# A hybrid decoder trunk on one NeuronCore: output projection and second norm by pairs of row tiles, and one list schedule to the end

## The chip, the cores and the metric

The kernel runs on one core of a Trainium2 chip. The metric is the device time of one execution in microseconds. A profiled execution gives a trace; its span is the time between the first and the last instruction in it.

## The reference

One layer on x of 1024 rows (tokens) by 1024 columns, all in float32:

```python
h = rms_norm(x, norm_mix)
xa, ga, q, f, v, g, m_a, m_b = split(h @ w_in)            # eight groups of 1024 columns
y_a = rg_lru(conv(xa)) * gelu(ga)                         # a gated linear recurrence over the rows
y_b = rms_norm(hgrn2(silu(q), f, v), hg_norm) * silu(g)   # 8 heads, a recurrence with a 128x128 state
y = sigmoid(m_a) * y_a + sigmoid(m_b) * y_b
x = x + y @ w_out                                         # the output projection
h = rms_norm(x, norm_mlp)                                 # the second norm
x = x + square(relu(h @ w_up)) @ w_down                   # w_up 1024x4096, w_down 4096x1024
out = rms_norm(x, norm_final)
```

## The kernel before

**Stages.** Columns stand on partitions in the mixer, rows (tokens) in the output projection. (1) The first norm and the projection of v. (2) The mixer: 28 quads, blocks of 256 columns of w_in, each multiplied in 7 products instead of 8 (a scheme after Strassen over two halves of the rows, two of the contraction and two of the columns), beside it the recurrences of `gated_recurrence` (4) and `hgrn` (8 heads), and `merge(u)`, which makes y of 128 columns, `u`, in two halves of 512 rows, `c`, and stores it to DRAM as `y_d[u, c]`. (3) The output projection `y @ w_out` with the residual, and the second norm, its result transposed and split into the seven operands of the MLP. (4) UP: 16 quads of w_up, 84 matmuls each (`hidden`), whose results go to DRAM. (5) DOWN: 8 rounds (`kb`) of two quads of w_down, added to eight accumulators `acc`, and the last norm.

**Exact products.** A float32 operand is split into a rounded high part H on ACT (`A.copy`) and a rest L on VectorE (`split`); a product is three matmuls, H by H, H by L and L by H (`mm3`).

**Weights.** A tile of w_out (two blocks of 128 rows by 512 columns) is 512 KB. It goes through one of three raw buffers and is split into one of three pairs H and L. `next_w` walks a fixed list, `seq`: the eight tiles three times, 24 loads and splits.

**Stage 3 before.** Row tiles are 128 rows; `tt` numbers them within a half of 512 rows, `t` over both (0 to 7), `hf` is a half of the 1024 result columns. First the first half: `load_y(0)` brings eight y tiles of 512 KB, four row tiles together accumulate in four PSUM banks over eight blocks `ku`, once for each `hf`, and the sums with x go to DRAM (`x2d`). Then `load_y(1)`, and in two parts: two row tiles of the first half are read back (`x2a`) and normed, then two row tiles of the second half are projected and normed. The norm of a row tile is a square with its sum (ACT), a power (POOL), a scaling (VectorE, `xn`), eight transposes (`xT_h`, TensorE), copies out of PSUM (`braw`), and splits; once both halves are there, `combos` makes the four combined operands. In PSUM there are four banks `pj`, two `sc`, two `hg`.

**What sets the order.** In the mixer each instruction is noted by class `Later` rather than issued: `note` finds what it depends on, `cost` estimates its length, `ordered` walks forward in estimated time and takes on each engine the ready instruction with the earliest due time, and `issue` emits the list. Each engine runs its queue in order, and SP's queue of DMAs too. From stage 3 on, before, the framework's scheduler orders the instructions by program order and priority.

**Memory.** Before, each stage opens pools of its own, and the mixer's tiles (its operands `hop`) are closed ahead of stage 3.

Of the kernel before, what the change touches and what calls it, by code (L numbers as in the profile page):

```python
# [11 lines left out]
F32 = mybir.dt.float32  # L12
F32R = mybir.dt.float32r
U8 = mybir.dt.uint8
AF = mybir.ActivationFunctionType
# [4 lines left out]
P = 128  # L20
# [36 lines left out]
class Later:  # L57
# [7 lines left out]
    TABLE = 1.28  # L65
# [11 lines left out]
    class Pool:  # L77
        def __init__(self, later, real):
            self.later, self.real = later, real

        def tile(self, shape, dtype, *, tag, name, bufs=1, **k):
            t = self.real.tile(shape, dtype, tag=tag, name=name, bufs=bufs, **k)
            ring = self.later.rings.setdefault((id(self), tag), [])
            ring.append(t.tensor.name)
            if len(ring) > bufs:
                self.later.before[ring[-1]] = ring[-1 - bufs]
            return t

    def __init__(self, tc):
        self.tc, self.on, self.due = tc, False, 0.0  # L90
        self.rings, self.before = {}, {}
        self.ops, self.seen, self.of_tile = [], {}, {}
# [10 lines left out]
    def cost(engine, method, out, k, aps):  # L103
# [14 lines left out]
        if engine == "POOL":  # L118
            return (0.2 + 0.00075 * n if method == "memset" else 0.65 + 0.0009 * n), 0.12, 0
# [30 lines left out]
    def ordered(self):  # L150
# [5 lines left out]
        for name, before in self.before.items():  # L156
            if name in self.of_tile and before in self.of_tile:
# [3 lines left out]
                preds.append(set(self.of_tile[before]))  # L161
# [53 lines left out]
        while done < total:  # L215
# [22 lines left out]
        self.span, self.starts = max(free.values()), starts  # L238
# [12 lines left out]
def trunk(ctx: ExitStack, tc: tile.TileContext, x, wts, quads, pv, gains, mask_f, mask_u, out):  # L251
    nc = tc.nc
    later = Later(tc)
# [10 lines left out]
    wp, rawp, ps = (Later.Pool(later, p) for p in (wp, rawp, ps))  # L264
    dram = ctx.enter_context(tc.tile_pool(name="dram", bufs=1, space=DRAM))

    def opened(name, **how):
        cm = tc.tile_pool(name=name, bufs=1, reuse_waits="tile", **how)
        return Later.Pool(later, cm.__enter__()), lambda: cm.__exit__(None, None, None)
# [7 lines left out]
    seq = [*range(V_TILES), *range(V_TILES)] + [*range(out0, out0 + OUT_TILES)] * 3  # L277
# [21 lines left out]
    def split_w(i, raw):  # L299
        h = wp.tile([P, 1024], F32R, tag="w", name=f"wH{i}", bufs=6)  # L300
        lo = wp.tile([P, 1024], F32R, tag="w", name=f"wL{i}", bufs=6)
# [38 lines left out]
    def gain_tile(i, pool):  # L340
        g = pool.tile([P, D], F32, tag="gain", name=f"gain{i}")
        nc.scalar.dma_start(g, gains[i : i + 1, :].to_broadcast([P, D]))
# [79 lines left out]
    def quad_steps(i, pools, raws=raw_tile, singles=2, adding=False):  # L422
# [38 lines left out]
        def pair(src, names):  # L461
            def go():
                h, lo = (pools[1].tile([P, 1024], F32R, tag="w", name=f"w{names[0]}{i}{q}", bufs=6) for q in "HL")
# [14 lines left out]
            "b": pair(lambda: s[0], ("s1", "s2")),  # L478
            "c": pair(lambda: s[1], ("s3", "s4")),
            "d": pair(lambda: raw[1], ("A12", "A22")),  # L480
# [10 lines left out]
    FAR = ("t1L", "n2L", "T3L", "T4L")  # L491
    hop = {
        o: [
            (hopr if o + q in FAR else hopl).tile([P, 4, T], F32R, tag=o + q, name=f"h{o}{q}") for q in ("H", "L")
        ]
        for _, _, o in PLAN
    }
# [574 lines left out]
    later.on = True  # L1072
# [28 lines left out]
    ysp, close_ys = opened("ys")  # L1101
# [3 lines left out]
    n2p, close_n2 = opened("n2")  # L1105
    gain1 = gain_tile(1, n2p)
# [349 lines left out]
```

## Time and profile before

| | us |
|---|---|
| median of 3 runs | 1633.67 (1632.45 to 1635.85) |
| profiled execution | 1640.74 |
| its span | 1639.0 |
| TensorE busy | 1551.2, 8520 matmuls |
| VectorE / ACT / POOL busy | 1232.0 / 859.8 / 273.2 |
| moved by DMA | 320.98 MB, mean 196 GB/s |

In the profile, PE is TensorE's matmuls, PEld its weight loads, DVE VectorE, ACT ScalarE, POOL GpSimd and SPq the DMA issues of SyncE. A name such as `po<-wH,y` is the output tile and the inputs, without numbers: `po` is a bank of the output projection, `wH` and `wL` a split weight tile, `y` a tile of y, `mga`, `mgb`, `mgo`, `mgh` the tiles of `merge`, `yd`, `od`, `hd`, `mad`, `mbd` tensors in DRAM, `uX`, `uY`, `uZ` the banks of UP, `dX` and so on those of DOWN. A row of busy time by stretch gives its start and end, its length, then the busy time of each engine with the instructions that lie in it, the granted clock of TensorE as a share of full speed, the busy share of the DMA engines, and GB/s.

### The profile page before, as it was taken

To read this page: it belongs to the slowest core of one execution; us is meant where nothing else is said; L and a number is where in the kernel's file an instruction comes from. 1 tells how busy PE (TensorE), PEld (TensorE's weight loads), DVE (VectorE), ACT (ScalarE), POOL (GpSimd) and SP (SyncE) were. 2 spreads that over 40 slices of the span, in tenths; PEclk is the share of its full clock that TensorE was granted. 3 is DMA by queue.
4 is the path that set the end of the run, shared out by engine and by line. 5 is a ranking of instruction groups with operands and counts; after the bars stand their busy time and mean duration, and the time that the engine had idled before them with its cause. 6 is when DMAs were issued, how large, how long until landed. Compare 5 with 4: busy or idle time off the path is not lost.

```text
span 1639.0 us, 22939 instructions
## 1 busy us (share of the span) xinstructions
PE 1551.2 (95%) x8520; PEld 1238.0 (76%) x8520; DVE 1232.0 (75%) x1780; ACT 859.8 (52%) x1356; POOL 273.2 (17%) x281
## 2 busy tenths in 40 slices
PE   5999999999999999988898797999999999999997
PEld 4787878777778777776776575878778878888886
DVE  4754586978778778877892387977777888788876
ACT  4643666468455854488542266766766732222113
POOL 0001222334214522345232000000000000000000
PEclk9999999999999999998899898999999999999999
DMA  5546464565564565545558861666656575666652
GB/s 189 168 130 181 127 200 121 169 190 171 155 171 152 168 201 170 169 148 148 168 178 292 296 227 67 261 250 233 232 222 239 219 295 211 256 252 244 256 206 103
DMA packets 110801, 320.98 MB, mean 196 GB/s; under 512 B 11872, under 2 KB 20192, under 8 KB 99936
## 3 DMA queue, kind: packets, MB, share of 16 engines
q1 hardware_dynamic: 101040, 299.05, 51.2%
q0 software_dynamic: 8064, 14.68, 5.8%
q10 hardware_dynamic: 1584, 5.77, 1.0%
q8 instruction: 67, 1.10, 0.3%
q14 instruction: 46, 0.38, 0.1%
HBM read 217.75 MB, written 101.71 MB: 195 GB/s over the span
## 4 chain that ended last, share of the span: by engine, by line
PE 74%; DVE 9%; DMA 7%; ACT 6%; issue 3%; POOL 1%; SPq 0%; DVEq 0%; POOLq 0%; ACTq 0%
PE pQFX L247 5%; PE pGMX L247 5%; PE pGAX L247 4%; PE dX L327 4%; PE dX L329 4%; PE dX L328 4%; PE uX L327 3%; PE uX L328 3%; PE uX L329 3%; PE pGMY L247 3%; DMA raw<-wts_in 2%; PE pQFY L247 2%; PE sc L247 2%; PE pGAY L247 2%; PE dY L329 2%
## 5 line engine op out<-in xcount | busy, mean ns | idle before, releaser
L1371 DVE TENSOR_TENSOR acc<-acc,dX 128x512 f32<-128x512 f32 x128 | 85.2, 683 | 31.0 <-PE dX L329 29.9
L288 ACT CAST wA<-q 128x512 fp32r<-128x512 f32 x33 | 20.4, 621 | 139.4 <-PE dX L329 102.7
L289 DVE TENSOR_TENSOR wL<-raw,wH 128x1024 fp32r<-128x1024 f32 x40 | 49.9, 1250 | 31.7 <-ACT wH L288 29.0
L247 POOL DMA_DIRECT2D s<-quads_in x52 | 46.6, 901 | 158.7 <-DMA s<-quads_in 46.0
L288 ACT CAST wH<-raw 128x1024 fp32r<-128x1024 f32 x40 | 41.9, 1047 | 44.2 <-PE po L328 18.7
L247 ACT ACT_TABLE_LOAD x50 | 64.2, 1283 | 1.6 <-PE pi L247 0.7
L327 PE MATMUL po<-wH,y 128*128 128x512 f32 x128 | 52.1, 410 | 4.7 <-DMA y<-yd 4.7
L1371 DVE TENSOR_TENSOR acc<-acc,dY 128x512 f32<-128x512 f32 x64 | 43.5, 685 | 16.2 <-PE dY L329 15.4
L247 DVE TENSOR_TENSOR s<-s,q 128x512 f32<-128x512 f32 x54 | 43.5, 806 | 11.6 <-DMA s<-quads_in 8.1
L328 PE MATMUL po<-wL,y 128*128 128x512 f32 x128 | 52.1, 407 | 0.0
L329 PE MATMUL po<-wH,y 128*128 128x512 f32 x128 | 51.3, 402 | 0.0
L1230 ACT ACTIVATE b<-b 128x512 f32<-128x512 f32 x48 | 30.3, 631 | 37.4 <-DVE b L1229 37.4
L247 DVE TENSOR_TENSOR qb<-qb,seg 128x512 f32<-128x512 f32 (+1 forms) x40 | 27.3, 683 | 17.0 <-PE sc L247 16.2
L247 DVE TENSOR_TENSOR kk<-kk,seg 128x768 f32<-128x768 f32 (+1 forms) x32 | 29.3, 915 | 9.3 <-PE sc L247 9.3
L247 PEld LDWEIGHTS sc<-qb,kk 128*32 128x32 f32 (+1 forms) x896 | 21.3, 116 | 19.7 <-issue 16.6
L289 DVE TENSOR_TENSOR wA<-q,wA 128x512 fp32r<-128x512 f32 x33 | 22.6, 686 | 14.9 <-ACT wA L288 14.9
L327 PEld LDWEIGHTS po<-wH,y 128*128 128x128 f32 x128 | 25.1, 197 | 10.5 <-DMA y<-yd 5.3
L247 PE MATMUL sc<-qb,kk 128*32 128x48 f32 (+2 forms) x896 | 27.3, 211 | 4.8 <-DVE dd L247 2.4
L1231 ACT ACTIVATE b<-b 128x512 f32<-128x512 f32 x48 | 30.2, 631 | 1.3
L247 POOL TENSOR_SCALAR scT<-dd 32x256 f32<-32x256 f32 x32 | 19.9, 621 | 60.8 <-DVE dd L247 48.0
L1150 PE MATMUL xT_h<-ident,xn_h 128*128 128x128 f32 x64 | 10.7, 323 | 20.0 <-DVE xn_h L351 13.0
L329 PEld LDWEIGHTS po<-wH,y 128*128 128x128 f32 x128 | 25.2, 197 | 5.4
(3093 smaller groups left out, 5502.1 us busy)
## 6 DMA issues: line engine op xcount, KB each, us to landing
q<-quads_in SPq DMA_DIRECT2D x92, 512.0 KB, 4.5
raw<-wts_in SPq DMA_DIRECT2D x40, 512.0 KB, 4.7
s<-quads_in SPq DMA_DIRECT2D x56, 256.0 KB, 2.9
s<-quads_in POOLq DMA_DIRECT2D x56, 256.0 KB, 5.0
y<-yd SPq DMA_DIRECT2D x16, 512.0 KB, 5.9
q<-quads_in SPq DMA_DIRECT2D x28, 256.0 KB, 4.0
x<-x_in SPq DMA_DIRECT2D x8, 512.0 KB, 4.6
vd<-vt SPq DMA_DIRECT2D x16, 256.0 KB, 3.6
```

Source lines behind the costliest of these rows:

```text
L247: go(*a, **k)
L288: keep(A.copy(h, src))
L289: keep(V.tensor_tensor(out=lo, in0=src, in1=h.bitcast(F32), op=ALU.subtract))
L327: PE.matmul(o, ah, bh, start=first, stop=False, **how)
L328: PE.matmul(o, ah, bl, start=False, stop=False, **how)
L329: PE.matmul(o, al, bh, start=False, stop=last, **how)
L1150: PE.transpose(pt[:, k * P : (k + 1) * P], xn[:, (4 * h + k) * P : (4 * h + k + 1) * P], ident)
L1230: A.activation(b[:, at, :], b[:, at, :], AF.Relu, scale=-1.0 if at == 2 else 1.0)
L1231: A.activation(b[:, at, :], b[:, at, :], AF.Square)
L1371: V.tensor_tensor(out=dst, in0=dst, in1=banks[bk, pr], op=op)
```

## The change

1. `later.issue()` moves from the end of the mixer to the end of the kernel: mixer, output projection, second norm, UP and DOWN are noted and ordered in one list. New due times: `OUT_FROM` 690 and 12 us a pair, 2.85 a step in UP, 1.4 a step and row pair in DOWN.
2. Homes of 8 KB last from the mixer to the end. Tiles of the mixer's operands (`NEAR`) give their places to later tiles of the same pool: B11H, B11L and t1H to y (three homes, later the u tiles), n2H to x (later the sums of the quads), B21H to the gain and xn, B21L and T3H to `braw` (later UP's results, then four accumulators). `Pool.place` and `before` follow which tiles share bytes.
3. The output projection goes by pairs of row tiles, `tt` and `tt + 4`, one of each half, with both `hf` for a pair before the next. y comes in 64 loads of 128 KB (rows of 512 bytes) instead of 16 of 512 KB; x in 8 of 512 KB. The sums are normed from where they lie, and stored to DRAM for DOWN; they are not read back. The last pair finishes its first row tile ahead of its second.
4. Weight tiles of w_out are kept in three homes by last use (`w_of`); pairs walk the tiles back and forth. Loads and splits remain 24.
5. Estimates: a DMA takes 1.9 us and its size at 330 GB/s (190 before), 160 with accumulation; POOL's costs are new; SP is held when more than 3 us of transfers are under way by the estimate (`AHEAD`).

The diff, cut to its core:

```diff
-    TABLE = 1.28
+    TABLE, AHEAD = 1.28, 3.0
...
-            slow = "accum_op" in k
-            return (0.92 if engine == "POOL" else 0.06), 1.9 + size / (1.0e5 if slow else 1.9e5), size / 2.0e5
+            moved = size / (1.6e5 if "accum_op" in k else 3.3e5)
+            return (0.92 if engine == "POOL" else 0.06), 1.9 + moved, moved
...
                 moving = max(moving, at) + moved
+                free[e] = max(free[e], moving - self.AHEAD)
...
+    NEAR = {"B11H": "y0", "B11L": "y1", "t1H": "y2", "n2H": "x2", "B21H": "gx", "B21L": "b0", "T3H": "b1"}
...
+    near = Homes(y=("y0", "y1", "y2"), x2=("x2",), gx=("gx",), b=("b0", "b1"), u1=("gx",), u2=("y0", "y1", "y2"), s=("x2",))
...
-    later.issue()
-    for close in (close_m, close_w1m, close_hopl, close_ev, close_hopr, close_mk):
+    for close in (close_m, close_w1m, close_ev, close_hopr, close_mk):
         close()
...
+    gx = near.tile([P, 2, D], F32, tag="gx", name="gx")
+    gain1, xn = gx[:, 0, :], gx[:, 1, :]
+    HIDDEN_PACE, DOWN_PACE, OUT_PACE, OUT_FROM = 2.85, 1.4, 12.0, 690.0
+    def w_of(hf, j):
+        if (hf, j) not in out_w:
+            home = used_at.index(min(used_at))
...
+            raw = load_w(i)
+            pair = [wp.tile([P, 1024], F32R, tag=f"w{home}{q}", name=f"w{q}{i}_{made[0]}") for q in "HL"]
+            split(raw, *pair)
...
-    ys = load_y(0)
-    for hf in range(2):
-        pp = out_proj(ys, hf, range(4), "0")
-        for tt in range(4):
-            cols = slice(hf * 512, (hf + 1) * 512)
-            xs = n2p.tile([P, D], F32, tag="xn", name=f"xs{tt}{hf}", bufs=2)[:, 0:512]
-            SP.dma_start(xs, x[tt * P : (tt + 1) * P, cols])
-            V.tensor_tensor(out=xs, in0=pp[tt], in1=xs, op=ALU.add)
-            SP.dma_start(x2d[tt][:, cols], xs)
-    ys = load_y(1)
-    for part in range(2):
-        tts = (2 * part, 2 * part + 1)
-        for tt in tts:
...
-            second_norm(tt, 0)
-        for hf in range(2):
-            pp = out_proj(ys, hf, tts, "1")
...
-        for tt in tts:
-            SP.dma_start(x2d[4 + tt], x2s[tt])
-            second_norm(tt, 1)
+    later.due = OUT_FROM
+    for tt in range(4):
+        js = range(4) if tt == 0 else range(3, -1, -1)
+        for n, u in enumerate([2 * j + k for j in js for k in range(2)]):
+            if n % 4 == 0:
+                yt = near.tile([P, 4, 2, 2, P], F32R, tag="y", name=f"y{u // 4}{tt}")
+            ys[u] = yt[:, u % 4]
+            for c in range(NC):
+                SP.dma_start(ys[u][:, c].bitcast(F32), y_d[u, c].rearrange("p (a t) -> p a t", a=2)[:, :, cut])
...
+        for i in range(2):
+            hf = (i + tt) % 2
+            alone = (tt, i) == (3, 1)
+            js = range(4) if i or tt == 0 else range(3, -1, -1)
+            for c_ in ((0,), (1,)) if alone else ((0, 1),):
+                for n, j in enumerate(js):
+                    later.due += OUT_PACE / 8 * len(c_)
+                    wh, wl = w_of(hf, j)
...
+                for c in c_:
+                    added_to(xs[c], hf, pp[c])
+                    if i:
+                        SP.dma_start(x2d[tt + 4 * c], xs[c])
+                        second_norm(tt + 4 * c, xs[c])
...
     def raw_mlp(name):
-        if name[0] == "s" and name[-1] == "1":
-            return w1p.tile([P, 1024], F32, tag="raw", name=name)
+        if name[0] == "s":
+            if name[-1] == "0":
+                sums_of[name[:-1]] = near.tile([P, 2, 1024], F32, tag="s", name=name)
+            return sums_of[name[:-1]][:, int(name[-1]), :]
         return raw_tile(name)
```

Three places in the order. The numbers that close a name tell buffers apart.

TensorE, where the projection comes to head 7's y. `po000` is the bank of column half 0, row tile 0 before; `y70` is y of head 7, first half of the rows; what follows is column half 1 from head 0 on.

```order
L327 MATMUL po003_8011<-wH15_8056,y70_7999 128x512
L328 MATMUL po003_8011<-wL15_8057,y70_7999 128x512
L329 MATMUL po003_8011<-wH15_8056,y70_7999 128x512
L327 MATMUL po010_8160<-wH16_8086,y00_7992 128x512
L328 MATMUL po010_8160<-wL16_8087,y00_7992 128x512
```

After, the names are `po`, pair, column half, half of the rows; `y10` holds heads 4 to 7 of pair 0, both halves, `y11` those of pair 1.

```order
L291 MATMUL po011_2088<-wH17_22_2090,y00_2067 128x512
L291 MATMUL po000_2073<-wH15_20_2082,y10_2068 128x512
L291 MATMUL po000_2073<-wL15_20_2083,y10_2068 128x512
L291 MATMUL po000_2073<-wH15_20_2082,y10_2068 128x512
L291 MATMUL po110_2108<-wH19_24_2096,y11_2105 128x512
L291 MATMUL po110_2108<-wL19_24_2097,y11_2105 128x512
L291 MATMUL po110_2108<-wH19_24_2096,y11_2105 128x512 x2
L291 MATMUL po110_2108<-wL19_24_2097,y11_2105 128x512
L291 MATMUL po110_2108<-wH19_24_2096,y11_2105 128x512
L291 MATMUL po001_2074<-wH15_20_2082,y10_2068 128x512
L291 MATMUL po001_2074<-wL15_20_2083,y10_2068 128x512
L291 MATMUL po001_2074<-wH15_20_2082,y10_2068 128x512
```

Pair 0's 66 other matmuls now stand ahead of head 7's y of the first half; behind it stand six of pair 1, and then head 7's y of the second half, with all the rest behind it. Before, the second half of the rows came only after 192 matmuls on the first.

SP's queue at the last merge, head 7 (`yd70` and `yd71` are its y in DRAM, `mg..70` and `mg..71` the tiles of its two halves). Before:

```order
L1116 DMA y60_7998<-yd60_190 128x1024
L247 DMA yd70_192<-mgb70_2027 128x512
L247 DMA yd70_192<-mga70_2025 128x512
L296 DMA raw17_8114<-wts_in 128x1024
L247 DMA mgo71_2030<-od7_159 128x512
L247 DMA mgh71_2028<-hd7_151 128x512
L1116 DMA y70_7999<-yd70_192 128x1024
```

After (`y01` is heads 0 to 3 of pair 1, in the home of `y00`):

```order
L291 DMA y01_2106<-yd10_180 128x2x128
L291 DMA y01_2106<-yd11_181 128x2x128
L291 DMA yd70_192<-mgb70_2027 128x512
L291 DMA raw13_2118<-wts_in 128x1024
L291 DMA yd70_192<-mga70_2025 128x512
L291 DMA mgo71_2030<-od7_159 128x512
L291 DMA mgh71_2028<-hd7_151 128x512
L291 DMA y10_2068<-yd70_192 128x2x128
L291 DMA y11_2105<-yd70_192 128x2x128
L291 DMA mgb71_2031<-mbd7_175 128x512
L291 DMA yd71_193<-mgb71_2031 128x512
L291 DMA yd71_193<-mga71_2029 128x512
```

The last two of eight `y01` loads, which wait for the home of `y00`, are now ahead of the store of the last merge's first half.

TensorE, from the last norms to UP. Before, row tiles 3 and 6 are transposed one behind the other when all the projection is done:

```order
L329 MATMUL po113_8721<-wH19_8742,y71_8307 128x512
L1150 MATMUL xT_h3_0_8628<-ident_69,xn_h3_8620 128x128 x4
L1150 MATMUL xT_h3_1_8636<-ident_69,xn_h3_8620 128x128 x4
L1150 MATMUL xT_h6_0_8792<-ident_69,xn_h6_8786 128x128 x4
L1150 MATMUL xT_h6_1_8798<-ident_69,xn_h6_8786 128x128 x4
L327 MATMUL uX0_8936<-h2B11H_7978,wA1128_8923 128x512
```

After, `po301` is the last bank (row tile 7) and `gx` holds xn:

```order
L291 MATMUL po301_2188<-wH12_40_2190,y03_2164 128x512
L291 MATMUL xT_h3_0_2186<-ident_69,gx_2066 128x128
L291 MATMUL xT_h3_1_2187<-ident_69,gx_2066 128x128
L291 MATMUL xT_h3_0_2186<-ident_69,gx_2066 128x128
L291 MATMUL xT_h3_1_2187<-ident_69,gx_2066 128x128
```

Row tile 6 has been transposed 60 matmuls earlier, and row tile 3's transposes follow the 24 matmuls of row tile 7.

More of the change, by code (lines that the diff above doesn't have):

```diff
@@ new lines, in before @@
+    def before(self):
+        where, last, names = {}, {}, {}
+        for pool, home, name in self.tiles:
+            if (pool, home) in last:
+                yield name, [last[pool, home]]
+            elif pool.side:
+                if pool not in where:
+                    lo, size = pool.place()
+                    where[pool] = (lo, lo + size)
+                lo, hi = where[pool]
+                yield name, [x for q, (a, b) in where.items() if q is not pool and a < hi and lo < b for x in names[q]]
+            last[pool, home] = name
+            names.setdefault(pool, []).append(name)
@@ L1142, in second_norm @@
-        norm_rows(xs, xn, gain1, f"h{t}")
+            braw[tt] = near.tile([P, 4, T], F32, tag="b", name=f"braw{t}")
+        b = braw[tt][:, 2 * half : 2 * half + 2, :]
+        norm_rows(xt, xn, gain1, f"h{t}")
         def op_split(src, o):
```

208 lines of the change are left out of this document (122 added, 86 removed).

## The prediction

> **What bounds the kernel now.** I read the page's span first, then the busy time by stage, then finer slices of the one stage that stands out, then TensorE's waits there. The first view is busy time by stretch: start and end, length, busy PE, PEld, DVE, ACT and POOL (with counts), granted clock, DMA share, GB/s.
>
> ```profile
> span 1639.0 us, 22939 instructions
> ```
>
> ```profile
> 100.00:720.00 620.00, 611.02 (x4052) 486.68 (x4050) 459.06 (x695) 355.71 (x599) 197.33 (x199) 0.99 0.57 166
> 720.00:855.00 135.00, 118.77 (x919) 92.45 (x918) 119.22 (x179) 89.27 (x139) 53.29 (x49) 0.90 0.51 158
> 855.00:1004.00 149.00, 118.46 (x531) 95.85 (x530) 85.32 (x121) 67.22 (x118) 15.90 (x16) 0.90 0.73 246
> 1004.00:1320.00 316.00, 311.00 (x1323) 248.22 (x1322) 248.79 (x307) 213.77 (x299) 0.00 (x0) 0.99 0.60 226
> 1320.00:1631.00 311.00, 309.95 (x1342) 250.92 (x1340) 252.49 (x370) 72.95 (x104) 0.00 (x0) 1.00 0.59 229
> 1375.00:1400.00 25.00, 25.00 (x111) 20.39 (x110) 18.33 (x27) 7.55 (x8) 0.00 (x0) 1.00 0.44 168
> ```
>
> TensorE is the bound: mixer body and MLP keep it busy 98 to 100% of the time at full clock. A full-speed matmul of 512 columns costs 25 / 110 = 0.227 us (one of the 111 had begun before the slice). The stage that the change rewrites, 855 to 1004, is the loose one: 30.5 us idle, and a mean clock of 0.90. The same matmuls in finer slices (busy PE, clock, DMA share, GB/s):
>
> ```profile
> 885.00:889.00 4.00, 1.10 (x5) 0.86 0.58 218
> 889.00:895.00 6.00, 6.00 (x16) 0.53 0.90 289
> 895.00:922.00 27.00, 26.69 (x118) 1.00 0.91 309
> 922.00:934.00 12.00, 0.31 (x2) 0.64 0.87 298
> 934.00:939.00 5.00, 5.00 (x17) 0.50 0.82 287
> 979.00:985.00 6.00, 1.87 (x12) 0.87 0.57 204
> 985.00:990.00 5.00, 2.67 (x12) 0.50 0.47 170
> 990.00:1000.00 10.00, 5.72 (x29) 0.99 0.18 57
> ```
>
> and TensorE's waits between 850 and 1025 (in all, times, longest):
>
> ```profile
> PE xT_h L1150 <- DVE xn_h L351: 13.0, 4, 12.0
> PE xT_h L1150 <- DVE rstd_h L349: 6.6, 2, 5.5
> PE po L327 <- DMA y<-yd: 4.7, 2, 2.9
> PE uZ L327 <- ACT braw L1151: 3.5, 1, 3.5
> ```
>
> There are three holes. At 885 the projection waits 2.9 us for the last y tile of the first half. At 922 it stands 11.7 us: the first transposes of the second norm wait for xn_h, whose input is written to DRAM and read back, and the second half's matmuls are queued behind. From 979 the last norms leave 4.1, 2.3 and 4.3 us empty, 10.7 in all. After each long hole the clock is 0.50 to 0.64 for some 5 us: the 16 matmuls of the six microseconds from 889 are 26 at full speed.
>
> **What the stage needs.** By 1004 the old kernel has done 384 projection matmuls and 26 of the MLP (counted in its order), 410 x 0.227 = 93.1 us. The 64 transposes come in eights:
>
> ```profile
> 959.22 1.06 PE L1150 MATMUL xT_h<-ident,xn_h 128*128 128x128 f32 x8 [1.02 <-DVE rstd_h L349]
> ```
>
> 8 x 1.06 = 8.5 us. The count of every matmul is the same after the change (the two orders have 7386 PE instructions each), and so are the 24 weight tiles to load and split. What the change can win here is at most the remainder of the 149 us, less some 7 us for the mixer's last small matmuls: about 40 us.
>
> **What the change removes.** The hole of 11.7 us goes: rows of the first half are no longer written out and read back before their norm, and three of the four pairs have the next pair's 96 matmuls (22 us) over their norm. The wait on the first y tile (the other part of the 4.7 us) goes too, as its home is free when the mixer's last B11 product is done.
>
> **What it adds: the last y, both halves, at once.** Pair 0 needs y of head 7 for rows 0 to 127 and 512 to 639. Before, the second half's y was wanted only after 922. Its birth is in the queues of SP, POOL and DVE:
>
> ```profile
> 875.79 0.42 SPq L1116 DMA_DIRECT2D y<-yd  x1
> 878.17 0.32 SPq L247 DMA_DIRECT2D yd<-mga  x1
> 882.34 0.32 SPq L247 DMA_DIRECT2D mgh<-hd  x1
> 888.27 0.32 SPq L247 DMA_DIRECT2D mgb<-mbd  x1
> 895.05 0.33 SPq L247 DMA_DIRECT2D yd<-mga  x1
> ```
>
> ```profile
> 886.98 1.26 POOL L247 TENSOR_TENSOR mga<-mga,mgh 128x512 f32<-128x512 f32 x1 [10.21 <-DMA mgh<-hd]
> 892.36 1.28 POOL L247 TENSOR_TENSOR mga<-mga,mgb 128x512 f32<-128x512 f32 x1
> ```
>
> The merge has three buffers, so the second half's loads wait for the first half's stores: store 878.2, landed 882.3; h loaded by 887.0; product, b loaded by 891.0, two products, cast, subtraction, store 895.1. That is 16.9 us from store to store. Three things move it. Two weight splits (wL of tiles 13 and 14) that stood ahead of head 7's state on VectorE now stand behind it,
>
> ```profile
> L289 DVE TENSOR_TENSOR wL<-raw,wH 128x1024 fp32r<-128x1024 f32 x22 | 26.8, 1223 | 22.1 <-ACT wH L288 22.1
> ```
>
> worth up to 2.4 us; I take 1.5. Against that, SP's eight y01 loads for pair 1 now stand ahead of that store; the first of them waits until TensorE has finished the y00 tile, and issuing eight costs 8 x 0.42 = 3.4 us. So the first store comes at 878.2 - 1.5 + 3.4 = 880. While TensorE waits the queue is emptier than at 0.9 share; I take 2 us off the 16.9. Then the y must land and be read in pieces of 128 KB. Nearest rows (KB each, median us to landing):
>
> ```profile
> od<-ot SPq DMA_DIRECT2D x16, 256.0 KB, 2.3
> vd<-vt SPq DMA_DIRECT2D x16, 256.0 KB, 3.6
> yd<-mga SPq DMA_DIRECT2D x16, 256.0 KB, 4.0
> y<-yd SPq DMA_DIRECT2D x16, 512.0 KB, 5.9
> raw<-wts_in SPq DMA_DIRECT2D x40, 512.0 KB, 4.7
> ```
>
> The store is 4.0. The load lies between 2.3 and 5.9; vd has the same 512-byte rows but twice the size, so 3.0. The last y stands at 880 + 14.9 + 7 = 902, with 894 to 913 as bounds (every transfer at its shortest or its longest row).
>
> Until then TensorE has only 75 projection matmuls to do by its new order: 42 of pair 0's first column half, 24 of its second, 9 more on rows of the first half. The chain of waits shows where the mixer's last projection ends:
>
> ```profile
> 855.05 0.76 PE pGAY L247 x4
> ```
>
> From 856 the 75 take 17 us, with the mixer's small ones to about 878. So some 24 us stand empty, less the 2 of the nine, where three holes were before. From 902:
>
> - 384 - 75 = 309 matmuls, 70.1 us; 64 transposes, 8.5; the 26 of the MLP, 5.9.
> - Half clock after the wait: the row at 889 lost 10 matmuls, 2.3; I take 2.
> - Weights and x: 24 tiles are needed, five or six a pair, one each 2.7 us in the bursts. A load of 4.7, a cast and a split of 1.2 with three raw buffers come every 2.3 us. That just holds, and cached tiles give 8 us of rest between; 3 (0 to 10).
> - The end: row tile 3's norm has 24 matmuls (5.5 us) over it, row tile 7's has eight transposes and eight matmuls, and its t1 17 more (3.9 us). What is left are a copy, a square and a cast between xT_h3 and the first MLP matmul, and t1 after xT_h7:
>
> ```profile
> L1151 ACT COPY braw<-xT_h 128x512 f32<-128x512 f32 x16 | 8.8, 587 | 8.0 <-PE xT_h L1150 8.0
> L348 ACT ACTIVATE xn_h<-x2s 128x1024 f32<-128x1024 f32 x4 | 4.2, 1050 | 0.0
> L288 ACT CAST h2B11H<-braw 128x512 fp32r<-128x512 f32 x4 | 2.5, 621 | 0.1
> ```
>
> 2 x 0.59 + 1.05 + 0.62 = 2.9, and about 2 for t1; 5 against 10.7 (3 to 9).
>
> 902 + 70.1 + 8.5 + 5.9 + 2 + 3 + 5 = 996.5 against 1004: **7.5 us won**, of a possible 40.
>
> **The rest.** Mixer up to 855: the same instructions, order changed by a few places at either end, by some tens in the middle, where TensorE is full; 0 (-5 to +5). The MLP now stands in the same list. Two waits stood there, with a slow clock after the second:
>
> ```profile
> PE uX L327 <- ACT e L1226: 4.1, 2, 2.4
> 1209.00:1212.00 3.00, 0.68 (x3) 0.59 (x4) 2.74 (x3) 3.00 (x4) 0.00 (x0) 1.00 0.08 36
> 1212.00:1215.00 3.00, 3.00 (x9) 2.40 (x8) 1.97 (x3) 1.48 (x3) 0.00 (x0) 0.52 1.01 415
> ```
>
> A copy of a PSUM bank stood on ACT behind a cast that waited for a quad's load. The sums have a home of their own now and a quad's load is issued a quad ahead, so these go: up to 6 us. A list made from estimated costs can put others in; I take 3 won (-6 to +6). DOWN is full at 0.23 us a matmul and gives nothing. Sum: 7.5 + 3 = 10.5. The profiled run was 1640.7 (span 1639.0 and 1.7 around it), 7 above the median of 1633.7, so I carry the difference over: **1623**.
>
> **The rivals.** A measurement can tell about 0.2%, 3.3 us, from no change.
>
> *The tail is shorter than I think* (0.23). Had the transfers their short rows, the last y would stand at 894; with 3 us at the end and all 6 us of the MLP that makes 1623 - 8 - 2 - 3 = 1610. For it: the queue is quiet while TensorE waits. Against: od<-ot alone reaches 2.3.
>
> *DMA becomes the bound* (0.10). From 902 on some 20.75 MB are still to move by SP's order, 4.25 of them y in rows of 512 bytes. At 309 GB/s at a share of 0.91 that is 61 us at full share, of some 95; were the y rows twice as slow, 74. So no, unless latencies stretch as at 0.9 share; a tile every 3.4 us for 16 tiles would add 11: 1634, no change. The Trainium skill, "DMA: Bandwidth & Descriptors", section "Measured (HBM→SBUF, 128 partitions, SWDGE, issued from GpSimd)", says to batch transfers to 1 MiB or more and shows 138 GB/s at 64 KB; by an estimate of mine from that page the 4.25 MB would take some 25 us and speak against quarter-size y loads. vd<-vt at 3.6 beside yd<-mga at 4.0 does not show that penalty.
>
> *The list gives the gain back* (0.08). If the estimated costs leave one 0.45 us wait in each of 24 rounds of the MLP, the 10.5 us are gone: 1633, no change. For it: engines run in order, and a DMA in the estimate is shorter than the rows above. Against: before, that stage waited 4 us in 300.
>
> *Slower: SP's line holds the merge* (0.17). The y01 loads wait for TensorE, TensorE for the split of the weight tiles of columns 512 up, that split for a raw load in SP's line. ACT's and DVE's last merge steps stand behind the same split. If these loads take the longest rows (y<-yd 5.9 and up) instead of 4.7, each link adds 2 to 4 us before the merge goes on, and the last y stands at 916 or later; with 4 us more for starved weights afterwards that is 1623 + 14 + 4 = 1641. It decides from a last y of 916 on.
>
> **The numbers.** My forecast has 0.42, its own range 1616 to 1630. Faster: 0.42 + 0.23 = 0.65; same: 0.10 + 0.08 = 0.18; slower 0.17. The range goes from the low end of the short tail to the slower case, 1607 to 1640.
>
> **What would show it.** Right: no read-back hole; TensorE empty from about 878 to about 902, broken by nine matmuls, and released by a y load; then 22 to 24 us a pair; about 5 us empty before the first MLP matmuls; no wait on e in the MLP. Wrong: a last y far from 902, holes on wH or raw between the pairs, or a wait that repeats in every round of the MLP.

## The result and the profile after

The changed kernel takes **1675.97 us** (median of 4 runs, 1672.99 to 1681.01); the kernel before, run beside it, 1633.06. The ratio is 1.0267, 95% interval 1.0231 to 1.0302: 43 us slower. The forecast of 1623 and its range up to 1640 are missed. The profiled execution took 1673.4 us.

Stretches of the changed kernel in the columns of the prediction's first view; from 855 on their bounds are others, as the stages lie later (start and end, length, busy PE, PEld, DVE, ACT and POOL with counts, granted clock, DMA share, GB/s):

```profile
span 1671.6 us, 22981 instructions
```

```profile
100.00:720.00 620.00, 593.88 (x3901) 467.83 (x3900) 438.23 (x679) 339.16 (x558) 192.66 (x189) 0.98 0.54 160
720.00:855.00 135.00, 119.42 (x769) 95.19 (x768) 117.99 (x170) 95.96 (x161) 61.52 (x52) 0.96 0.56 165
855.00:900.00 45.00, 44.17 (x432) 34.59 (x432) 33.47 (x60) 23.39 (x56) 10.83 (x11) 1.00 0.82 271
900.00:1004.00 104.00, 76.49 (x333) 60.54 (x332) 52.54 (x70) 40.42 (x61) 9.66 (x11) 0.87 0.63 210
1035.00:1350.00 315.00, 311.46 (x1334) 249.47 (x1332) 249.39 (x309) 217.24 (x304) 0.00 (x0) 1.00 0.62 235
```

The first row is the surprise. In the mixer's body TensorE had been busy for 611.0 of 620 us; now it is busy for 593.9. Seventeen microseconds are gone before the rewritten stage begins. The stage itself has the picture that was predicted, later: TensorE's instructions around the last y (start, length, then what ended the idle time before it),

```profile
900.90 0.39 PE L291 MATMUL po<-wH,y 128*128 128x512 f32 x1
917.26 0.79 PE L291 MATMUL po<-wH,y 128*128 128x512 f32 x1 [15.97 <-DMA y<-yd]
922.01 0.63 PE L291 MATMUL po<-wH,y 128*128 128x512 f32 x1
929.58 0.79 PE L291 MATMUL po<-wH,y 128*128 128x512 f32 x1 [6.94 <-DMA y<-yd]
```

TensorE stands from 901 to 929.6, broken by nine matmuls, and each half ends with a y load; predicted were 878 and 902. Its waits from 850 to 1040 (in all, times, longest):

```profile
PE po L291 <- DMA y<-yd: 23.5, 3, 16.0
PE xT_h L291 <- DVE gx L291: 2.6, 1, 2.6
PE uX L291 <- ACT h2B11H L291: 2.5, 1, 2.5
```

The read-back is gone from the list, and so is the 13.0 on `xn_h`. How late the mixer ends is read in SP's queue, where the last head's output `ot` is stored, first before the change,

```profile
873.60 0.32 SPq L247 DMA_DIRECT2D od<-ot  x1
```

then after, with what follows there:

```profile
894.96 0.32 SPq L291 DMA_DIRECT2D od<-ot  x1
...
902.19 5.11 SPq L291 DMA_DIRECT2D y<-yd  x8
...
908.50 0.41 SPq L291 DMA_DIRECT2D yd<-mga  x1
```

It is 21.4 us late, and the eight loads of `y01` stand for 5.1 us ahead of the last merge's first store. The account, in the spans of the profiled executions, against what was predicted (1639.0 less 10.5, 1628.5):

| piece | predicted | measured | lost |
|---|---|---|---|
| mixer, to the last `od<-ot` | 873.6 | 895.0 | 21.4 |
| from there to the last y | 28.4 | 34.6 | 6.2 |
| last y to the 26th matmul of the MLP (counted in the order) | 94.5 | 103.3 | 8.8 |
| from there to the end | 632.0 | 638.7 | 6.7 |

That is the 43.1 us between 1628.5 and 1671.6. The remaining 10 of the 53 between 1623 and 1676 are how the two profiled runs lie to their medians: before 7 above, after 2.6 below. Part of those 7 stands in the mixer: three runs further down have the mixer's order of the kernel before, and their last `od<-ot` comes at 869.0, 870.4 and 873.0. The 21.4 is therefore rather a low figure, and two profiles of the same order can lie some 5 us apart.

**Why the mixer is late** shows first in what VectorE waits for between 100 and 855. Before:

```profile
DVE s L247 <- DMA q<-quads_in: 3.4, 2, 1.7
DVE s L247 <- DMA s<-quads_in: 8.1, 4, 3.3
```

After:

```profile
DVE s L291 <- DMA q<-quads_in: 25.6, 13, 5.8
DVE s L291 <- DMA s<-quads_in: 10.5, 3, 9.0
```

`s` are the sums of a quad's blocks, `q` its loads. The wait on `s` itself is little longer than before; the wait on `q` is what grew, by 22 us. In thirteen places a sum now stands in VectorE's queue ahead of its load's landing, and everything behind it in that queue comes late, the splits that TensorE needs among it:

```profile
PE pGMX L291 <- DVE ws124L L291: 7.3, 1, 7.3
PE pXAZ L291 <- DVE wA120L L291: 4.5, 1, 4.5
PE pQFZ L291 <- DVE wA1211L L291: 3.8, 1, 3.8
```

The theory (A): the new estimates in `cost` made the mixer's order late. The rival (C): the one list to the end, or the lasting homes, did. For the stage behind it, theory B: SP's line holds the last merge.

### The profile page after: what moved, and what is told of

The parts are those of the page before. It is cut to its first block, busy times and chain, and to the rows that moved or that the text cites. A ratio compares the mean times of both kernels' runs of the same rounds, so it can differ in the third digit from the quotient of the medians.

```text
span 1671.6 us, 22981 instructions
## 1 busy us (share of the span) xinstructions
PE 1557.3 (93%) x8520; PEld 1237.8 (74%) x8520; DVE 1225.9 (73%) x1780; ACT 858.8 (51%) x1355; POOL 282.2 (17%) x281
## 5 line engine op out<-in xcount | busy, mean ns | idle before, releaser
L291 DVE TENSOR_TENSOR s<-s,q 128x512 f32<-128x512 f32 x118 | 83.6, 709 | 38.8 <-DMA q<-quads_in 25.6
L291 PE MATMUL po<-wH,y 128*128 128x512 f32 x256 | 80.2, 410 | 26.9 <-DMA y<-yd 23.5
L291 DVE TENSOR_TENSOR wA<-q,wA 128x512 fp32r<-128x512 f32 x59 | 42.4, 719 | 8.4 <-ACT wA L291 8.4
L291 PE MATMUL uX<-h2B11H,wA 128*128 128x512 f32 x128 | 44.4, 407 | 2.5 <-ACT h2B11H L291 2.5
L291 DVE TENSOR_TENSOR wL<-raw,wH 128x1024 fp32r<-128x1024 f32 x24 | 29.1, 1221 | 16.6 <-ACT wH L291 16.5
L291 ACT CAST wH<-raw 128x1024 fp32r<-128x1024 f32 x24 | 25.2, 1049 | 31.2 <-PE po L291 11.5
L291 POOL TENSOR_TENSOR mga<-mga,mgh 128x512 f32<-128x512 f32 x16 | 26.7, 1671 | 54.1 <-DMA mga<-mad 28.6
L291 PEld LDWEIGHTS po<-wL,y 128*128 128x128 f32 x128 | 24.6, 196 | 10.1 <-DVE wL L291 5.7
L291 PEld LDWEIGHTS uX<-h2B11H,wA 128*128 128x128 f32 x128 | 24.7, 194 | 8.7 <-ACT h2B11H L291 2.9
L291 PEld LDWEIGHTS sc<-qb,kk 128*32 128x32 f32 (+1 forms) x896 | 20.0, 114 | 14.9 <-issue 11.7
L291 POOL TENSOR_TENSOR mgb<-mgb,mgo 128x512 f32<-128x512 f32 x16 | 23.9, 1494 | 31.4 <-DMA mgo<-od 13.3
```

Source lines behind the costliest of these rows:

```text
L291: go(*a, **k)
```

## Experiments

### The estimates, as a whole

In the changed kernel, all of the old `cost` and no holding of queues:

```diff
-            moved = size / (1.6e5 if "accum_op" in k else 3.3e5)
-            return (0.92 if engine == "POOL" else 0.06), 1.9 + moved, moved
+            slow = "accum_op" in k
+            return (0.92 if engine == "POOL" else 0.06), 1.9 + size / (1.0e5 if slow else 1.9e5), size / 2.0e5
...
-            t = {"memset": 0.2 + 0.00075 * n, "tensor_tensor": 0.4 + 0.0023 * n}.get(method, 0.6 + 0.0005 * n)
-            return t + 0.5 * (scalars > 0), 0.12, 0
+            return (0.2 + 0.00075 * n if method == "memset" else 0.65 + 0.0009 * n), 0.12, 0
...
-                free[e] = max(free[e], moving - self.AHEAD)
```

> The changed kernel, ordered by the estimates of the kernel before (DMA, POOL) and with SP not held. Theory A, that the new estimates make the mixer's order late (in the changed kernel VectorE stands 25.6 us in 13 waits for the quads' loads, before 3.4 in 2): the mixer comes back by some 17 us, the wait on the last y stays, so 1650 to 1662 against 1676. Theory C, that the one list to the end or the lasting homes slow the mixer whatever the estimates: 1672 to 1680.

Then the first of these alone, and the second alone:

> The changed kernel with only the DMA estimate of before (1.9 us and the size at 190 GB/s); POOL's new costs and the holding of SP stay. If the DMA estimate carries the mixer's slip (theory A1): as with all old estimates, 1650 to 1662. If POOL's new costs carry it (theory A2), or the long list (C): 1672 to 1680.

> The changed kernel with only POOL's costs of before. Theory A2 (POOL's new costs move VectorE's and POOL's work onto one another, where a split takes 2.2 us instead of 1.2): 1650 to 1662. Theories A1 and C: 1672 to 1680.

And the reverse: the kernel before with all three new estimates, nothing else.

> The kernel before, its mixer ordered by the new estimates and with SP held; nothing else changed. Theory A: the mixer loses here what it loses in the changed kernel, some 17 us: 1645 to 1655 against 1633. Theory C (the long list or the homes): 1630 to 1637.

Measured: old estimates in the changed kernel **1737.8** (ratio to the kernel before 1.0626, 1.0608 to 1.0644); old DMA estimate alone 1725.3 (1.0554, 1.0539 to 1.0570); old POOL costs alone 1678.7 (1.0268, 1.0253 to 1.0284), no change against the 1676 of the changed kernel. New estimates in the kernel before **1654.5** (1.0128, 1.0107 to 1.0148).

The last hits theory A: the estimates alone cost the old kernel 20 us. The first two miss every theory in the total, by 45 us and more, because two things happened at once. Busy time by stretch with all old estimates:

```profile
100.00:300.00 200.00, 194.86 (x1062) 154.80 (x1061) 121.78 (x192) 106.05 (x161) 45.03 (x48) 0.98 0.55 153
300.00:500.00 200.00, 197.64 (x1504) 155.85 (x1502) 162.42 (x256) 116.82 (x199) 66.73 (x69) 1.00 0.59 173
500.00:720.00 220.00, 216.87 (x1468) 173.56 (x1468) 173.54 (x259) 128.17 (x232) 78.80 (x78) 0.99 0.58 173
1035.00:1350.00 315.00, 291.83 (x1170) 228.61 (x1169) 212.51 (x262) 183.79 (x263) 0.00 (x0) 0.95 0.53 201
```

From 100 to 720 TensorE is busy for 609.4 us again (611.0 before, 593.9 after): the mixer is mended. But UP, which these estimates did not order before, now has 291.8 busy of 315 (311.5 after). UP moves 235 GB/s in the changed kernel; the old estimate lets DMA move 200. That a list which believes this puts UP's loads and casts wrong fits TensorE's longest wait there with the old DMA estimate alone, and was not tried apart:

```profile
PE uX L291 <- ACT wA L291: 14.0, 6, 7.6
```

### Old estimates in the mixer, new ones behind it

So the two were parted: operations noted before the output projection keep the old estimates and are not held.

```diff
-    later.due = OUT_FROM
+    later.due, later.late = OUT_FROM, len(later.ops)
```

(`cost` and the holding ask whether `late` is set.)

> The changed kernel, its mixer ordered by the estimates of before without the holding of queues, everything from the output projection on by the new ones. If the mixer's slip is the estimates' and the rest of the list is well served by the new ones: TensorE as far at 725 us as before (695 us of work, 679 in the changed kernel), 17 us come back: 1655 to 1662 against 1676. If the one long list itself holds the mixer: 1672 to 1680.

And on top of it a fence: the eight `y01` loads depend on the last merge's stores.

```diff
+                if tt == 1 and n >= 4:
+                    later.ops[-1][5].update(merged)
```

> As the one before, and the eight loads of pair 1's second y tile (y01) may stand in SP's queue only behind the stores of the last merge. Theory B (SP's line holds the merge: y01's loads wait for TensorE and take 5.1 us to issue, the last merge's loads and stores are queued behind): the last y comes 5 to 20 us sooner than without the fence, and the time falls by 4 to 12 us more. If the merge's own loads set its pace: within 3 us of the kernel without the fence.

Measured: **1650.6** (1.0105, 1.0084 to 1.0126), and with the fence 1650.4 (1.0097, 1.0077 to 1.0116). 25 of the 43 us are the mixer's estimates, and rival C is out for them: the one list and the lasting homes are all still there. The fence gives nothing in time. TensorE with the fence, around the last y:

```profile
891.80 0.79 PE L297 MATMUL po<-wH,y 128*128 128x512 f32 x1 [13.68 <-DMA y<-yd]
...
903.89 0.80 PE L297 MATMUL po<-wH,y 128*128 128x512 f32 x1 [6.72 <-DMA y<-yd]
```

With the mixer in time and the fence TensorE stands from 878.1 to 903.9; without the fence, which is the case that was predicted, from 879.0 to 906.3. Predicted were 878 and 902. So the fence brings the last y 2.4 us sooner in these two profiles. Theory B had forecast 5 to 20 us and 4 to 12 us of time; what came is the other forecast, that the merge's own loads set its pace. The store of the first half, `yd<-mga`, is issued at 885.91 without the fence and at 885.84 with it, so here the `y01` loads do not hold it. POOL's product ahead of that store waits for the merge's load. First before the change, then with the fence:

```profile
873.73 1.67 POOL L247 TENSOR_TENSOR mgb<-mgb,mgo 128x512 f32<-128x512 f32 x1 [4.72 <-DMA mgo<-od]
```

```profile
881.84 1.26 POOL L297 TENSOR_TENSOR mgb<-mgb,mgo 128x512 f32<-128x512 f32 x1 [7.44 <-DMA mgb<-mbd]
```

The load `mgb<-mbd` is issued at 867.6 before and at 874.4 with the fence. In the changed kernel itself the `y01` loads do hold the first half's stores, by some 3 us: ACT and VectorE have its two parts ready at 903.9 and 905.2, and `yd<-mgb` and `yd<-mga` are issued at 907.39 and 908.50, behind the eight loads and a weight load.

### Which estimate

In the kernel before, one new estimate at a time, DMA, POOL, the holding, and then a DMA estimate longer than the old one (`size / 1.4e5`, with accumulation 0.8e5):

> The kernel before, its mixer ordered with the new DMA estimate alone. All three new estimates together cost it 20 us (1654 against 1634). Theory A1: a 512 KB load stands at 1.9 + 1.6 = 3.5 us in the new estimate and takes 4.5 in the trace, so VectorE's sums of quads are put where the load is not yet in, and TensorE waits behind VectorE: 10 to 20 us slower, 1644 to 1654. Theory A2 (POOL's costs) or A3 (SP and POOL held by the new rule): 1631 to 1637.

> The kernel before, its mixer ordered with POOL's new costs alone. Theory A2: 1644 to 1654. Theories A1 and A3: 1631 to 1637 (putting POOL's old costs back into the changed kernel gained nothing).

> The kernel before, its mixer ordered with the queues held when over 3 us of transfers are under way by the estimate, and nothing else new. Theory A3 (the rule holds POOL's queue too, which issues the adding loads of the quads, so its products are put late): 1640 to 1654. Theory A1: 1631 to 1637.

> The kernel before, its mixer ordered with a longer DMA estimate than before: 512 KB in 5.6 us (4.7 before, 3.5 after, 4.5 in the trace). If a too short estimate is the fault (a load is taken to be there before it is): 1631 to 1640. If the order is only tuned to its estimates and any other costs 14 us: 1645 to 1652.

Measured: DMA 1648.0 (1.0085, 1.0056 to 1.0114); POOL 1650.4 (1.0089, 1.0058 to 1.0120); holding 1636.4 (1.0011, 0.9992 to 1.0029); longer DMA 1635.0 (1.0003, 0.9989 to 1.0017). The DMA estimate costs 14 us when it goes below the measured landing time and nothing when it goes above: 512 KB stand at 3.5 us in the new one, 4.7 in the old, 5.6 in the longer, and land in

```profile
q<-quads_in SPq DMA_DIRECT2D x92, 512.0 KB, 4.5
```

(The holding rule acts on every queue that issues DMAs, POOL's too, and costs nothing clear of noise.) VectorE's waits with the new DMA estimate in the old kernel are those of the changed kernel; with the longer one there is no such wait on `q` at that line. That the landing time is the part that costs fits this, but is not shown by itself: the new estimate also lets transfers follow one another faster, and no run has that part alone.

```profile
DVE s L247 <- DMA q<-quads_in: 31.1, 14, 6.6
```

POOL's costs cost as much, as theory A2 had it, although the run that put the old ones back into the changed kernel gained nothing. The two losses don't add (14 and 15 alone, 20 together). The end of the mixer, read at the last `od<-ot`, shows the same in both kernels, by one profile of each run:

| kernel | estimates in the mixer | last `od<-ot` |
|---|---|---|
| before | old | 873.6 (869.0 to 873.0 in three others) |
| before | new DMA | 887.9 |
| before | new POOL | 885.2 |
| before | all new | 890.9 |
| changed | all new | 895.0 |
| changed | new DMA, old POOL | 892.8 |
| changed | old DMA, new POOL | 885.6 |
| changed | all old, and behind it too | 877.7 |
| changed | all old, new behind it | 873.9 |

In either kernel one of the two new estimates alone is enough for more than half of the loss.

### POOL's costs taken apart

Of the new costs only tensor_tensor (`0.4 + 0.0023 * n`); all but it; then all of POOL at the mean durations of the trace; then tensor_tensor alone with the head's power at its measured 1.13:

> The kernel before, its mixer ordered with POOL's new cost for tensor_tensor alone (1.58 us for 512 columns, 1.11 before; the merge's products take 1.28 in the trace where VectorE is idle and 1.5 to 2.2 where it is not). POOL's new costs together cost 14.5 us. If this part carries it: 1643 to 1652, else 1631 to 1638.

> The kernel before, its mixer ordered with POOL's other new costs (tensor_scalar and copies of 512 columns 0.86 us, 1.36 with a column of scalars, 1.11 before); tensor_tensor as before. If a shorter estimate is again the fault, as with DMA: 1643 to 1652 and the run with the longer tensor_tensor alone at 1631 to 1638.

> The kernel before, its mixer ordered with POOL's costs set to the mean durations of its own trace (products of 512 columns 1.58 us, the power of the head's norm 1.13, the scalings of wi, wj and xp 2.05, the other tensor_scalar 0.4 + 0.0007 a column and 0.5 more with a column of scalars). If what hurts is a cost below the measured one (the new power stands at 0.41 us against 1.13 in the trace, the scaling of wi at 0.86 against 2.04): 1628 to 1637. If the old order is good by its tuning and not by its costs: 1643 to 1650, as with each part of the new costs.

> As the run with the longer tensor_tensor alone (1645.1), but the power of the head's norm, which that cost puts at 0.41 us, at its measured 1.13. If the too short power is what cost the 10 us: 1631 to 1637. If the longer products cost them: 1643 to 1648.

Measured: 1645.1 (1.0063, 1.0048 to 1.0078); 1645.5 (1.0064, 1.0047 to 1.0080); **1633.1** (0.9989, 0.9973 to 1.0005); 1642.9 (1.0045, 1.0028 to 1.0061). The durations of before, by shape (busy time, mean ns):

```profile
L247 POOL TENSOR_TENSOR mga<-mga,mgb 128x512 f32<-128x512 f32 x16 | 27.4, 1714 | 1.2
L247 POOL TENSOR_TENSOR hrs<-hssq,mhalf 128x4 f32<-128x4 f32 x16 | 18.1, 1131 | 65.9 <-DVE hssq L247 65.8
L247 POOL TENSOR_SCALAR wi<-wi 128x512 f32<-128x512 f32 x8 | 16.4, 2044 | 6.7 <-ACT wi L247 6.1
```

The new cost of a product, 1.58 us, is near the trace: the merge's three products take 1.71 (the first row), 1.53 and 1.51 us. For the power and the scaling the new costs are too short (0.41 and 0.86). The old costs are below the trace in all three (1.11, 0.65 and 1.11) and lose nothing, so "too short" is no rule for POOL. With all three near the trace nothing is lost either, so the old order is not good by tuning alone. (In that run's one profile the last `od<-ot` even comes at 860.9, but this execution, at 1628.6, is the fastest of ten, and the median gains nothing clear of noise.) But the half-right sets lose: products and power near the trace, with the rest as before, still cost 7 us, and that the power is the whole of it is refuted. VectorE's waits for POOL don't tell the sets apart. With all new POOL costs they are

```profile
DVE xd L248 <- POOL wi L248: 12.5, 4, 5.9
DVE xc L248 <- POOL xp L248: 9.1, 5, 3.1
```

against 2.6 and 1.1 before; but in the set that loses nothing they are 4.8 and 7.2, and in the one that loses 11 us (all but tensor_tensor) 5.7 and 5.4. Why a set loses that is nearer to the truth in one entry stays open.

### The rest: the seam from UP to DOWN

Behind the 26th matmul the changed kernel is 4.0 us slower than the kernel before, where 3 won were predicted. These are two pieces. The first product of DOWN starts at 1316.6 before and 1340.3 after. Before, 12 matmuls of UP (2.8 us) still stand behind it, after none. With them put to UP, it takes 315.1 and 307.4 us from that matmul, and DOWN 319.6 and 331.3: 7.7 won, 11.7 lost. TensorE's waits of the changed kernel at the seam:

```profile
PE dZ L291 <- DVE wA1258L L291: 2.6, 1, 2.6
PE dY L291 <- ACT ws159H L291: 2.0, 1, 2.0
```

The kernel with old estimates in the mixer has the same there. On it, the splits of DOWN's first two quads were made due earlier:

```diff
+        later.due -= 25.0
         for k in ("sums", "a", "b", "c", "d"):
             w_late[k]()
+        later.due += 25.0
```

(and 12 us for the other quad's).

> The changed kernel with the mixer's order by the old estimates (1650.6), and the splits of DOWN's first two quads due 12 and 25 us earlier. DOWN takes 334 us there, 322 before; TensorE waits 8 us in all for ws159, wA1258 and u0 between 1314 and 1360 and then runs 10 us at half clock. If these late splits are DOWN's loss: 6 to 9 us less, 1641 to 1645. If the loads (1.00 of the DMA engines' time at the seam) or the memory they wait for are the bound: 1648 to 1653.

Measured: 1651.5 (1.0102, 1.0082 to 1.0122), nothing won. The named waits went and others came, the longest for the addition to an accumulator, which frees the bank:

```profile
PE dX L297 <- DVE acc L297: 4.9, 1, 4.9
```

VectorE is busy for 9.97 and 9.47 of the ten microseconds from 1310 and from 1320, and this addition stands in its queue behind splits that were put earlier. A full VectorE is not the reason by itself: in the kernel before it is busy for 10.00 and 9.96 there, and TensorE waits for it 0.5 us in all at the seam. So the lateness of these splits is not the whole of it; which order would serve the seam stays open.

UP's gain in the kernel before, by asking for a quad's load a step earlier:

> The kernel before, with the load of the next quad in UP asked for one step earlier (ahead of a quad's first step). If UP's two waits on e, 4.1 us and 3 us of slow clock behind the second, come of that load's place in the order: 3 to 7 us less, 1627 to 1632. If the raw buffers keep the load back: 1632 to 1637.

Measured: 1633.5 (0.9998, 0.9987 to 1.0008), nothing. TensorE still waits for `e` twice, 3.8 us in all; the load's place in the program did not move these waits.

### The hole of before, filled

The prediction called the hole at 922 an order on TensorE. In the kernel before, the first half's norms moved behind the next 48 matmuls:

```diff
-            second_norm(tt, 0)
         for hf in range(2):
             pp = out_proj(ys, hf, tts, "1")
+            if hf == 0:
+                for tt in tts:
+                    second_norm(tt, 0)
```

> The kernel before, with the norms of the first half's row tiles written behind the projection of the first column half of the second half's rows instead of ahead of it: 48 matmuls, 11 us, stand over the read-back. If the hole of 11.7 us (and the 2.3 us of half clock behind it) is no more than an order on TensorE, 10 to 14 us go: 1620 to 1625. If the second half's y or its weights are not there by then, the wait changes its name: 1630 to 1636.

Measured: 1634.0 (0.9984, 0.9967 to 1.0001), no change. The wait stayed where it was, 13.1 us, and changed its name:

```profile
PE po L327 <- ACT wH L288: 13.1, 1, 13.1
```

The cast waits for a weight load, and SP issues that load only after the stores of the first half's sums, which wait for TensorE's last matmuls:

```profile
924.49 0.96 SPq L1169 DMA_DIRECT2D x<-xs  x2
...
926.05 1.49 SPq L296 DMA_DIRECT2D raw<-wts_in  x3
```

So three weight loads were put ahead of them as well:

```diff
         pp = out_proj(ys, hf, range(4), "0")
+        if hf == 1:
+            raws.extend(load_w(seq[made[0] + q]) for q in range(3))
```

> The kernel before with the norms behind the first column half (as in the run that gained nothing, where TensorE stood 13.1 us for a weight tile in the same place), and with the next three weight tiles' loads put ahead of the first half's x, its stores and the second half's y in SP's queue. If the order of SP's queue keeps the hole open: the weights are split by 920, 9 to 14 us go, 1621 to 1627. If the transfers themselves are the bound from 890 to 935 (a DMA share of 0.9 to 1.0 at 300 GB/s): the 4 MB of y come later by as much, 1630 to 1636.

Measured: 1639.1 (1.0033, 1.0022 to 1.0043), slower by 5, outside both forecasts. The hole is smaller (6.5 us idle from 910 to 940), but TensorE now waits 11.6 us for y in five places, and the norms pushed back meet the last ones. From 970 to 1000 VectorE is full and TensorE is not:

```profile
970.00:980.00 10.00, 4.39 (x25) 3.31 (x25) 9.85 (x16) 6.14 (x13) 0.55 (x1) 0.95 0.21 68
980.00:990.00 10.00, 6.82 (x28) 5.41 (x28) 9.48 (x16) 6.67 (x14) 1.72 (x2) 0.70 0.23 91
990.00:1000.00 10.00, 2.89 (x6) 1.64 (x7) 9.57 (x15) 5.85 (x10) 0.00 (x0) 0.64 0.15 52
```

No run beat the kernel before.

## Why the prediction was wrong

**Mixer up to 855: "0 (-5 to +5)"** is the step that failed, with 21 of 43 us. It measured 21.4 us late at the mixer's end, and the old estimates in the mixer alone bring 25 us of time back. The text called it the same instructions with "order changed by a few places at either end, by some tens in the middle, where TensorE is full". The order had been read for the places, not for what the new costs say against the trace: 3.5 us for a load whose row, 4.5, was in the trace. POOL's new costs, 0.41 us for a power of 1.13, stood beside it and cost the old kernel as much alone. That comparison belonged under the estimates' rival, which named it ("a DMA in the estimate is shorter than the rows above"), gave it 0.08, and looked for it in the MLP only. A full TensorE was cover only while VectorE, in order, ran ahead of it; with 13 waits for loads that stand too early in its queue it no longer did.

**The last y, both halves, at once** had the right picture, and a time that came out near by some luck. With the mixer in time, and without the fence, the last y is read at 906.3 (902 predicted, 894 to 913 as bounds) and the pause begins at 879.0 (878 predicted). But the terms err both ways. The first store comes at 885.9, not 880, and not for the `y01` loads: POOL waits for the merge's own load, which the text had taken as the kernel before has it. From store to store it is 15.7 us instead of 14.9, and from the last store to the read y 4.7 instead of 7. In the changed kernel the eight `y01` loads hold SP's line for 5.1 us, not 3.4; a 128 KB load lands in

```profile
y<-yd SPq DMA_DIRECT2D x64, 128.0 KB, 2.9
```

against 3.0 taken. The Trainium skill, "DMA: Bandwidth & Descriptors", section "Measured (HBM→SBUF, 128 partitions, SWDGE, issued from GpSimd)", speaks against such small transfers. Here they land in half the median time of the 512 KB loads of y before (2.9 against 5.9 us); what they cost is SP's issue time, 0.64 us each.

**After the last y: 103.3 us for 94.5.** The 309 matmuls, 64 transposes and 26 matmuls of the MLP were put at 84.5 us of work, half clock at 2, weights and x at 3, the end at 5. The row from the last y to the 26th matmul:

```profile
929.60:1032.90 103.30, 92.14 (x400) 73.54 (x401) 69.70 (x94) 52.17 (x81) 5.28 (x8) 0.92 0.60 204
```

Busy are 92.1, so slow clock costs some 7.6 instead of 2: it comes after the pause and again after the end's two waits. Idle are 11.2 instead of 8: the end is right (2.6 on `gx`, 2.5 on `h2B11H`), and weights, x and y are 6.

**The MLP: "3 won (-6 to +6)"** was 4.0 lost. The wait on `e` is gone as said, and UP wins 7.7 us. "DOWN is full and gives nothing" overlooked that its beginning is now ordered by the same list: it loses 11.7.

**The rivals.** "SP's line holds the merge" had the right side and decided from a last y of 916 on; it came at 929.6. But its mechanism is worth some 3 us, at the first store of the changed kernel; the mixer was already 21.4 us late when the line began. That it had the right side was luck. Of the 6.2 us that the merge is late against the text, the rest was not taken apart by a run; with the mixer in time the merge's own load made its first store 5.9 us later than predicted. "DMA becomes the bound" didn't happen: the share from 900 to 1004 is 0.63.

**The 11.7 us hole, "goes"**, did go, and was worth less than its length. The runs on the kernel before show why: with the order mended it is held by SP's queue, and with that mended TensorE waits for y and, by the rows from 970 to 1000, for VectorE's norms.

## What to carry to other kernels

Where a change touches a list scheduler's costs, set each new cost against the measured duration first, ask which in-order engine will stand behind an operation put too early, and run the old kernel with the new costs alone: here that showed 20 us. A set of costs that is good for one stage need not be for the next: the new ones cost the mixer 20 us, and the old ones cost the stages behind it far more (1737.8 against 1650.6). A hole on the busiest engine can have a second and a third cause under the first: before counting its length as a gain, look at what the next engine does in it.

## What the runs showed of the hardware

VectorE and POOL slow each other down in operations with two tensor inputs, so that the duration of one depends on what the other does. In the changed kernel, VectorE around the split of `wA1211L`, the one that TensorE waited 3.8 us for:

```profile
411.93 1.27 DVE L291 TENSOR_TENSOR_SCAN wi<-ej,hcar,wi 128x512 f32<-128x512 f32 x1
413.13 2.23 DVE L291 TENSOR_TENSOR_SCAN wj<-ej,hcar,wj 128x512 f32<-128x512 f32 x1
415.29 2.23 DVE L291 TENSOR_TENSOR wA1211L<-q,wA1211H 128x1024 fp32r<-128x1024 f32 x1
```

and POOL at the same time:

```profile
412.17 2.11 POOL L291 TENSOR_TENSOR mgb<-mgb,mgo 128x512 f32<-128x512 f32 x1 [0.49 <-DMA mgb<-mbd]
414.36 2.07 POOL L291 TENSOR_TENSOR mga<-mga,mgb 128x512 f32<-128x512 f32 x1
```

Alone the split takes 1.22 us and the product 1.27 (the prediction's rows), and the first scan, which ran when the product came, 1.27. Behind it each takes 2.1 to 2.2, and the ends come in turn, 413.20, 414.28, 415.36, 416.43 and 417.52, each some 1.08 us behind that of the other engine: one waits while the other works. The Trainium skill, "SBUF — State Buffer", section "Who interferes with whom", says that among the engines only the port pair shared by these two contends, as an exclusive lock; these rows agree.

And the clock falls after little idle time. TensorE's last matmul before the end's first wait is over by 1016.3, and it starts again at 1018.9:

```profile
1017.00:1018.00 1.00, 0.00 (x0) 0.00 (x0) 0.56 (x2) 0.08 (x1) 0.45 (x1) 1.00 0.28 111
1018.00:1019.00 1.00, 0.09 (x1) 0.12 (x2) 1.00 (x2) 0.54 (x1) 0.00 (x0) 0.64 0.00 0
1019.00:1020.00 1.00, 1.00 (x5) 1.00 (x6) 0.96 (x2) 0.00 (x0) 0.00 (x0) 0.50 0.06 16
```

Half clock sets in between 1018 and 1019, some 2 us after the last matmul, and stays for the next products, so even a wait of 2.6 us can have a slow restart in its price. How soon varies: with the old estimates in the mixer the same wait, also 2.6 us, has the granted clock at 1.00 up to the restart, at 0.70 in the microsecond behind it and then at 0.50. The Trainium skill, "TensorE: Matmul & The Clock Gate", section "What's actually happening", gives an idle window of about 3.4 us for this; in the rows above less was enough.
